# MLP down projection of a one-core layer: the seven block products as the outer loop, sums kept in PSUM, operand sums stored by the up stage

## The chip, the cores and the metric

The kernel runs on one core of a Trainium2 chip. The metric is the time of one execution on the device, in microseconds (us); three runs of the kernel before took 1432.04, 1435.4 and 1437.7 us, a median of 1435.4 us.

## The reference, cut to what matters

One layer over 1024 tokens of width 1024: an attention group and an mLSTM group share an input projection, their outputs go through one output projection, then an MLP of width 4096 and a gated embedding (PLE) follow, and a final norm.

```python
h = h + mix @ w_out[layer]
u = rms_norm(h, norm_mlp_g[layer])
h = h + jnp.square(jax.nn.relu(u @ w_up[layer])) @ w_down[layer]
gate = jax.nn.sigmoid(rms_norm(h, norm_ple_g[layer]) @ w_ple_gate[layer])
h = h + gate * (p[layer] @ w_ple[layer])
return rms_norm(h, final_norm_g)
```

## The kernel before, in words

Everything lies feature-major: a tile is 128 features by 1024 tokens, or by one half of them (512, `CH`). Each fp32 operand of a matmul is split into a high part (ACT's CAST, line 93, L93) and a low part (DVE's subtraction, L94), and each product is then three matmuls, L102 (high by high), L103 and L104 (`mm3`). A matmul is 128x128 by 512 columns.

The stages that matter here follow each other on PE in this order. The **out-projection** (tile `o`) has a first half on the attention output (`mixa`) and a second half on the mLSTM output (`mixm`, weights `wo_r`, loaded at L735 by `load_t`). The second half finishes `h[k]` feature block by feature block, stores it (L846, `hs<-h`), adds its square to `state` (L807/808) and scales it (L848). From the scaled `h`, `operands` makes the operands `x` of the up stage, four plain blocks and four sums `t` that POOL makes (L789). The **PLE product** `pl` (96 matmuls, operand `pp` from the load `pr` at L829) is independent of all that. `rstd_rows` turns `state` into a row factor: a column sum on PE (`cs`, L125), DVE (`ra`, L134), a power on POOL (`rb`, L135 and L823), a broadcast on PE (`bp`, L131), a copy on ACT (`rB`, L814).

The **up stage** (tile `u`, 1344 matmuls) and the **down stage** (tile `d`, 1344 matmuls) replace the eight block products of a 2x2 by 2x2 block matrix product by seven (Strassen-Winograd): `OPS = b11, t1, t2, b22, t3, b21, t4`. This needs sums of weight blocks, which POOL makes in `load_blocks` (L752 to 754) from a load of 512 KB (L751), and sums of operand blocks (`operands`). In the up stage, per pair of feature blocks `f` (16 of them), the result is `zz`: additions on DVE (L895), relu and scaling (L897), squaring on ACT (L898), and a store to DRAM of 1 MB (`zd<-zz`, L899).

The down stage loops over eight groups `g` of 512 hidden features, reads them back (`zr<-zd`, L870), makes the operand sums on POOL and the splits on ACT and DVE, and inside over four pairs of output blocks `o`. Each of the seven products of a pair `(g, o)` is six matmuls in a PSUM bank that is then added into `h` by DVE (L927, 208 times; 16 more go through ACT L924 and POOL L925). After the last group come `state` and the splits `hp` (L96/97), `rstd_rows` once more, and the **PLE gate** (tile `pg`, 456 matmuls, weights `wpg_r`), its evacuations (L947 to 950), the final norm and the output.

The order on each engine is set by a scheduler that runs over the recorded instructions; each engine then executes its list in order, and a DMA issue that waits on SP holds back all later issues of SP.

Of the kernel before, what the change touches and what calls it, by code (L numbers as in the profile page):

```python
# [9 lines left out]
F32 = mybir.dt.float32  # L10
# [35 lines left out]
def layer_kernel(ctx, tc, xT, wqk, wv, wvg, wmv, wmqk, wmo, wout, wup, wdown, wpg, wple, pT,  # L46
# [97 lines left out]
    zd = dram.tile([FF // P // 2, P, 2, T], F32, name="zd")  # L144
# [569 lines left out]
    with ExitStack() as tail:  # L714
        zp = tail.enter_context(tc.tile_pool(name="zp", bufs=2, reuse_waits="tile"))
        wta, wtb, wtc = [tail.enter_context(tc.tile_pool(name="wt" + n, bufs=2, reuse_waits="tile"))
                         for n in "abc"]
        pmm = tail.enter_context(tc.tile_pool(name="pmm2", bufs=6, space=PSUM, reuse_waits="tile"))

        def ztile(name, dt=F32):  # L720
            return zp.tile([P, 2, T], dt, name=name, tag="z", bufs=3)
# [4 lines left out]
        def acc_tile(name, tag="mm"):  # L726
            return pmm.tile([P, CH], F32, name=name, tag=tag, bufs=6 if tag == "mm" else 2)
# [5 lines left out]
        def load_t(src, name, n=KT * P, hl=None):  # L733
            raw = wtc.tile([P, 8 * L], F32, name=name + "_r", tag="wc")
            nc.sync.dma_start(raw[:, :n], src)  # L735
            hl = hl or [t.rearrange("p a b -> p (a b)") for t in wtile(name, 4, "wb")]
            return split([t[:, :n] for t in hl], raw[:, :n])
# [64 lines left out]
        def ssq(state, src, first, eng=V):  # L802
# [5 lines left out]
            eng.tensor_tensor(state, state, sq, op=ALU.add)  # L808

        def rows(dst, c):  # L810
            for j in range(NCH):
                bp = acc_tile("bp2", "x")
# [3 lines left out]
        def rstd_rows(state, times=None):  # L816
            cs = acc_tile("cs2", "x")
# [13 lines left out]
        state, scale = pair("state", F32)  # L831
# [8 lines left out]
        for k in range(KT):  # L840
# [6 lines left out]
            ssq(state, h[k], k == 0)  # L847
# [4 lines left out]
        rB = rstd_rows(state, srec)  # L852
# [13 lines left out]
        def hidden(f, halves=None):  # L866
            if halves is None:
                z = ztile("zr")
                halves = z[:, 0], z[:, 1]
                nc.sync.dma_start(z, zd[f])  # L870
            else:
                for i in range(2):
                    nc.sync.dma_start(halves[i], zd[f, :, i])
            return halves

        OWN = (0, 14, 15)
        for f in range(FF // P // 2):
            if f == FF // P // 2 - 2:
                ahead = [hidden(0), hidden(1, [unit("zr", F32) for _ in range(2)])]
# [19 lines left out]
            nc.sync.dma_start(zd[f], z)  # L899
# [3 lines left out]
        BY_POOL, POOL_O = ("t4",), (1, 2)  # L903
        hp = []
        count[0] = 0

        def operand():
            count[0] += 1
            return pair("y") if count[0] % 9 else (unit("y"), unit("y"))

        for g in range(NG):
            src = ahead if g == 0 else [hidden(2 * g + u) for u in range(2)]
            Y = operands(src, operand, lambda n: unit(n, F32))
            if g == 0:
                h = [unit("h", F32) for _ in range(KT)]
                for k in range(KT):
                    nc.sync.dma_start(h[k], hs[k])
            for o in range(KT // 2):
                def ev(key, ps):
                    i, c = dict(b11=(0, 0), t1=(1, 1), t2=(0, 1), b22=(0, 1), t3=(1, 1), b21=(0, 0), t4=(1, 0))[key]  # L920
                    to = h[2 * o + i][:, c * CH:(c + 1) * CH]
                    if key in BY_POOL and o in POOL_O:
                        t = small("t")
                        S.copy(t, ps)  # L924
                        G.tensor_tensor(to, to, t, op=ALU.add)  # L925
                    else:
                        V.tensor_tensor(to, to, ps, op=ALU.add)  # L927
                products([load_blocks(wdown[g, o], "wd")], [Y], ev, "d")
                if g == NG - 1:
                    for k in (2 * o, 2 * o + 1):  # L930
                        if k == 0:
                            state = pair("state", F32)[0]
                        ssq(state, h[k], k == 0, G if o < 3 else V)
                        hp.append(split((unit("hp"), unit("hp")) if k in (2, 3) else pair("hp"),
                                        h[k], col[:, C_GPLE + k:C_GPLE + k + 1]))
        rB = rstd_rows(state)


# [22 lines left out]
        def final(i, sl):  # L961
            n = sl.stop - sl.start
            nt = n // P
            cs = acc_tile("cs3", "x")
# [8 lines left out]
            bp = acc_tile("bp3", "x")  # L973
# [3 lines left out]
            for k in range(KT):  # L977
                m = 2 * T // n
                if k % m == 0:
                    outs = ztile("out").rearrange("p a (b t) -> p (a b) t", t=n)  # L980
# [14 lines left out]
        TO = ((4, 8), (4, 8), (2, 4, 6, 8))  # L995
        ws = {}

        def fetch(k):
            if k % 2 == 0:
                e = ztile("e")  # L1000
                nc.sync.dma_start(e, ed[k // 2])
                emb[k], emb[k + 1] = e[:, 0], e[:, 1]
            ws[k] = load_t(wpg[k], "wpg", hl=pair("wpg") if k == KT - 1 else None)

        for k in range(KT - LATE):
# [91 lines left out]
```

## Time and profile before

| what | value |
|---|---|
| median of 3 runs | 1435.4 us (1432.04 to 1437.7) |
| the profiled execution: own time / span | 1431.62 us / 1429.8 us |
| busy, share of the span: PE, DVE, ACT, POOL | 95%, 73%, 44%, 38% |
| PE busy | 1353.3 us, 6815 matmuls |
| traffic | 157.91 MB, mean 110 GB/s |
| chain that ended last, by engine | PE 44%, DVE 13%, POOL 8%, DMA 5%, issue 4% |

The span is the stretch that the profiler recorded; the own time is what the same execution took on the device. A matmul's duration in a row (about 0.39 us) is longer than its pitch, since matmuls overlap in the pipeline; the pitch is the distance of two starts. In the rows of a timeline the bracket at the end is the idle time of that engine before the instruction, and what ended it. The granted clock (PEclk) is a share of the full 2.4 GHz.

### The profile page before, as it was taken

The page shows a single profiled execution, that of the slowest core. Times are in us where ns is not written, and L with a number is a line of the kernel's source. Part 1 is how long each engine was busy: PE and PEld are TensorE (multiplying, and loading weights), DVE is VectorE, ACT ScalarE, POOL GpSimd, SP SyncE. Part 2 cuts the span into 40 slices and gives each one's busy share as a digit, 9 for nine tenths or more (in the row PEclk, how much of TensorE's full clock was granted, in tenths as well). Part 3 has the DMA queues.
Part 4 walks back from the last instruction along what each step waited for, and adds up shares of the span by engine and source line. Part 5 has one row for each costly group of instructions (what it writes and reads, how often), then busy time and mean ns, then how long its engine had stood idle before and what let it go on. Part 6 is the DMA issues. An engine that isn't in the chain of part 4 may idle for free.

```text
span 1429.8 us, 18360 instructions
## 1 busy us (share of the span) xinstructions
PE 1353.3 (95%) x6815; PEld 1123.4 (79%) x6815; DVE 1043.3 (73%) x1603; ACT 628.0 (44%) x1007; POOL 548.0 (38%) x395
## 2 busy tenths in 40 slices
PE   8999999999979999998999999997999899999996
PEld 6978988978868887777888888885777777777885
DVE  6788689599758894784444444459988899998666
ACT  6455645644455352355344333443433334335332
POOL 1532121141113220263332233348766878746002
PEclk9999999999999999999999999999999999999998
DMA  6111012222144368442432223446323133221403
GB/s 225 45 49 38 23 48 73 60 77 97 60 147 137 108 211 291 159 162 103 147 118 103 98 94 118 148 148 236 118 96 110 59 104 103 74 59 60 161 30 118
DMA packets 54233, 157.91 MB, mean 110 GB/s; under 512 B 5664, under 2 KB 15808, under 8 KB 49152
## 3 DMA queue, kind: packets, MB, share of 16 engines
q1 hardware_dynamic: 54144, 156.75, 32.4%
q8 instruction: 53, 0.87, 0.3%
q14 instruction: 36, 0.29, 0.1%
HBM read 113.19 MB, written 43.54 MB: 110 GB/s over the span
## 4 chain that ended last, share of the span: by engine, by line
PE 44%; DVE 13%; POOL 8%; DMA 5%; issue 4%; ACT 2%; SPq 0%; DVEq 0%; POOLq 0%; ACTq 0%
PE u L102 7%; PE u L103 7%; PE u L104 6%; POOL t L789 3%; PE d L102 2%; DVE h L927 2%; PE d L104 2%; DVE wdl L94 2%; PE d L103 2%; POOL wd_r L752 2%; PE pg L104 2%; PE pg L102 2%; PE pg L103 2%; DVE y L94 2%; DMA wd_r<-wdown 2%
## 5 line engine op out<-in xcount | busy, mean ns | idle before, releaser
L102 PE MATMUL d<-y,wdh 128*128 128x512 f32 x448 | 179.2, 403 | 18.9 <-DVE h L927 13.4
L94 DVE TENSOR_TENSOR wul<-wu_r,wuh 128x768 fp32r<-128x768 f32 (+1 forms) x64 | 75.3, 1178 | 148.9 <-ACT wuh L93 148.7
L103 PE MATMUL d<-y,wdh 128*128 128x512 f32 x448 | 178.1, 398 | 1.1 <-DVE y L94 1.1
L103 PE MATMUL u<-x,wuh 128*128 128x512 f32 x448 | 175.2, 395 | 0.0
L104 PE MATMUL d<-y,wdl 128*128 128x512 f32 x448 | 170.0, 400 | 4.9 <-DVE wdl L94 4.8
L102 PE MATMUL u<-x,wuh 128*128 128x512 f32 x448 | 172.3, 395 | 0.0
L104 PE MATMUL u<-x,wul 128*128 128x512 f32 x448 | 171.2, 394 | 0.0
L927 DVE TENSOR_TENSOR h<-h,d 128x512 f32<-128x512 f32 x208 | 132.9, 676 | 3.5 <-PE d L104 3.1
L752 POOL TENSOR_TENSOR wu_r<-wu_r 128x512 f32<-128x512 f32 x32 | 44.9, 1403 | 207.9 <-DMA wu_r<-wup 151.7
L102 PEld LDWEIGHTS d<-y,wdh 128*128 128x128 f32 x448 | 85.2, 190 | 47.0 <-DVE h L927 19.4
L93 ACT CAST wdh<-wd_r 128x1024 fp32r<-128x1024 f32 (+1 forms) x64 | 58.9, 942 | 130.8 <-POOL wd_r L753 89.4
L94 DVE TENSOR_TENSOR wdl<-wd_r,wdh 128x1024 fp32r<-128x1024 f32 (+1 forms) x64 | 89.5, 1404 | 26.0 <-ACT wdh L93 26.0
L104 PEld LDWEIGHTS d<-y,wdl 128*128 128x128 f32 x448 | 85.1, 190 | 28.1 <-DVE wdl L94 8.1
L103 PEld LDWEIGHTS d<-y,wdh 128*128 128x128 f32 x448 | 85.2, 190 | 20.8 <-DVE y L94 1.5
L104 PEld LDWEIGHTS u<-x,wul 128*128 128x128 f32 x448 | 84.7, 189 | 19.9
L103 PEld LDWEIGHTS u<-x,wuh 128*128 128x128 f32 x448 | 84.6, 189 | 19.9
L102 PEld LDWEIGHTS u<-x,wuh 128*128 128x128 f32 x448 | 84.5, 189 | 19.5
L93 ACT CAST wuh<-wu_r 128x768 fp32r<-128x768 f32 (+1 forms) x64 | 60.2, 942 | 74.9 <-POOL wu_r L753 45.7
L752 POOL TENSOR_TENSOR wd_r<-wd_r 128x512 f32<-128x512 f32 x32 | 49.6, 1552 | 72.0 <-DMA wd_r<-wdown 58.4
L412 ACT ACTIVATE pr<-pr,mn 128x128 f32<-128x128 f32 (+3 forms) x64 | 49.5, 774 | 54.6 <-PE av L415 30.4
L887 ACT COPY tmp<-u 128x512 f32<-128x512 f32 x48 | 28.0, 586 | 95.1 <-PE u L104 95.1
L407 DVE CUSTOM_DVE_ANT_0 pr<-s,biasS 128x512 f32<-128x512 f32 (+2 forms) x96 | 51.1, 550 | 12.5 <-PE tp L422 8.9
(363 smaller groups left out, 3712.1 us busy)
## 6 DMA issues: line engine op xcount, KB each, us to landing
wu_r<-wup SPq DMA_DIRECT2D x32, 512.0 KB
zd<-zz SPq DMA_DIRECT2D x16, 1024.0 KB
wd_r<-wdown SPq DMA_DIRECT2D x32, 512.0 KB
zr<-zd SPq DMA_DIRECT2D x15, 1024.0 KB
wm_r<-wmqk SPq DMA_DIRECT2D x8, 512.0 KB
wo_r<-wout SPq DMA_DIRECT2D x16, 256.0 KB
hs<-h SPq DMA_DIRECT2D x8, 512.0 KB
ed<-emb SPq DMA_DIRECT2D x4, 1024.0 KB
```

Source lines behind the costliest of these rows:

```text
L93: S.copy(hi, src)
L94: V.tensor_tensor(lo, src, hi.bitcast(F32), op=ALU.subtract)
L102: PE.matmul(ps, wh, xh, start=start, stop=False, skip_group_check=more)
L103: PE.matmul(ps, wh, xl, start=False, stop=False, skip_group_check=more)
L104: PE.matmul(ps, wl, xh, start=False, stop=stop, skip_group_check=more)
L407: V.tensor_tensor_reduce(pr[:, ks], s[:, :n], biasS[:, b0 + o:b0 + o + n], 1.0, -2 * LOW, op0=ALU.add, op1=ALU.min, accum_out=mn[:, o // C ...
L412: S.activation(pr[:, :nk], pr[:, :nk], AF.Exp, scale=-1.0, bias=mn[:, :1], accum_out=den)
L752: G.tensor_tensor(raw[:, 4:7:2], raw[:, 2:3].to_broadcast([P, 2, L]), raw[:, 1:4:2], op=ALU.subtract)
L789: G.tensor_tensor(ts[key][:, us], src[u][i0][:, s0], in1, op=o)
L887: S.copy(tmp[key], ps)
L927: V.tensor_tensor(to, to, ps, op=ALU.add)
```

## The change

The up stage computes the four operand sums of the down stage itself, on DVE, and stores them beside `z` (8 slots of half a token row per feature block instead of 2 rows of whole tokens). The down stage turns its loops round: the seven products are the outer loop, the eight groups the inner one, and per step it loads one operand tile `y_r` (512 KB) and one or two weight blocks `wd_r` (512 KB each, two for `t1` and `t3`), makes one weight sum on POOL for four of the seven products, splits both, and issues 24 matmuls into four PSUM banks. A bank collects its sums over all eight groups and is added into `h` only at the last (28 times). `state`, `hp` and the row factor are made for each half of the tokens, the second half's (`rstd_half(1)`) after `t3`. The out tiles and loads of the PLE gate take their buffers from the pools of the down stage. The pools before the down stage are laid out anew: `wtc` (raw weights of the out-projection and the up stage) comes right behind the small tiles, and `wtc`, `zu`, `wta` and `wtb` are closed after the up stage, so that the buffers of the down stage lie where they were. PSUM has one pool of eight banks in place of six and two.

```diff
-    zd = dram.tile([FF // P // 2, P, 2, T], F32, name="zd")
+    zd = dram.tile([FF // P // 2, P, 8, CH], F32, name="zd")
...
-        wta, wtb, wtc = [tail.enter_context(tc.tile_pool(name="wt" + n, bufs=2, reuse_waits="tile"))
-                         for n in "abc"]
-        pmm = tail.enter_context(tc.tile_pool(name="pmm2", bufs=6, space=PSUM, reuse_waits="tile"))
+        up_scope = ExitStack()
+        wtc, zu, wta, wtb = [up_scope.enter_context(tc.tile_pool(name=n, bufs=2, reuse_waits="tile"))
+                             for n in ("wtc", "zu", "wta", "wtb")]
+        pmm = tail.enter_context(tc.tile_pool(name="pmm2", bufs=8, space=PSUM, reuse_waits="tile"))
...
-            nc.sync.dma_start(zd[f], z)
+            nc.sync.dma_start(zd[f, :, :4], z.rearrange("p a (c t) -> p (a c) t", t=CH))
+            ts = ztile("zt").rearrange("p a (c t) -> p (a c) t", t=CH)
+            c0, c1 = slice(0, CH), slice(CH, T)
+            V.tensor_tensor(ts[:, 0], z[:, 0, c1], z[:, 0, c0], op=ALU.subtract)
+            V.tensor_tensor(ts[:, 1], z[:, 1, c1], ts[:, 0], op=ALU.add)
+            V.tensor_tensor(ts[:, 2], z[:, 0, c1], z[:, 1, c1], op=ALU.add)
+            V.tensor_tensor(ts[:, 3], z[:, 1, c0], ts[:, 1], op=ALU.subtract)
+            nc.sync.dma_start(zd[f, :, 4:], ts)
+        up_scope.close()
...
-        for g in range(NG):
-            src = ahead if g == 0 else [hidden(2 * g + u) for u in range(2)]
-            Y = operands(src, operand, lambda n: unit(n, F32))
...
-            for o in range(KT // 2):
...
-                        V.tensor_tensor(to, to, ps, op=ALU.add)
-                products([load_blocks(wdown[g, o], "wd")], [Y], ev, "d")
...
-        rB = rstd_rows(state)
+        rawp, hlp = [tail.enter_context(tc.tile_pool(name=n, bufs=3, reuse_waits="tile")) for n in ("rawp", "hlp")]
...
+        def parts(name, tag, src):
+            return split([hlp.tile([P, T], F32R, name=name + i, tag=tag + i) for i in "hl"], src)
+
+        def wraw(g, blk):
+            r = stream("wd_r", "wr", 4)
+            nc.sync.dma_start(r, wdown[g, blk])
+            return r
...
+        def weights(key, g):
+
+            if key in ("b11", "b21", "t4"):
+                return wraw(g, dict(b11=A11, b21=A12, t4=A22)[key])
+            if key == "t1":
+                a, b = wraw(g, A21), wraw(g, A22)
+                G.tensor_tensor(sw[g], a, b, op=ALU.subtract)
+            elif key == "t3":
+                a, b = wraw(g, A21), wraw(g, A11)
+                G.tensor_tensor(a, a, b, op=ALU.subtract)
+                return a
+            else:
+                a = wraw(g, dict(t2=A11, b22=A12)[key])
+                G.tensor_tensor(sw[g], a, sw[g], op=ALU.subtract)
+            return sw[g]
...
+        def ready(k, c):
+
+            sl = slice(c * CH, (c + 1) * CH)
+            if k == 0:
+                S.activation(state[:, sl], h[k][:, sl], AF.Square)
+            else:
+                sq = small("sq")
+                S.activation(sq, h[k][:, sl], AF.Square)
+                G.tensor_tensor(state[:, sl], state[:, sl], sq, op=ALU.add)
+            split((hp[k][0][:, sl], hp[k][1][:, sl]), h[k][:, sl], col[:, C_GPLE + k:C_GPLE + k + 1])
...
+        for key in OPS:
...
+            for g in range(NG):
+                y = stream("y_r", "yr", 3)
+                nc.sync.dma_start(y.rearrange("p (f t) -> p f t", t=CH),
+                                  zd[2 * g:2 * g + 2, :, SLOT[key]].rearrange("f p t -> p f t"))
+                yh, yl = parts("y", "y", y)
+                wh, wl = parts("wd", "w", weights(key, g))
+                for o in range(KT // 2):
+                    for u in range(2):
...
+                        mm3(ps[o], wh[:, at], wl[:, at], yh[:, us], yl[:, us],
+                            fresh and g == 0 and u == 0, g == NG - 1 and u == 1, not fresh)
+                    if g == NG - 1:
+                        to = h[2 * o + i][:, c * CH:(c + 1) * CH]
+                        V.tensor_tensor(to, to, ps[o], op=ALU.add)
+                        if key in DONE:
+                            ready(2 * o + i, c)
+            if key == "t3":
+                rstd_half(1)
+        rstd_half(0)
```

The order of the two programs at three places, engine by engine:

**Between the out-projection and the up stage.** SP's list before, around the load `pr` of the PLE operand; `wo_r` are the weights of the second half of the out-projection, `hd` and `in` its other traffic:

```order
L735 DMA wo_r<-wout 128x512 x2
L667 DMA hd<-t 128x512
L665 DMA t<-xT 128x512 x2
L667 DMA hd<-t 128x512
L844 DMA h<-hd 128x1024
L735 DMA wo_r<-wout 128x512
L540 DMA in<-mixmd 128x512
L735 DMA wo_r<-wout 128x512
L667 DMA hd<-t 128x512
L540 DMA in<-mixmd 128x512
L667 DMA hd<-t 128x512
L829 DMA pr<-pT 128x2x1024
```

and now:

```order
L845 DMA h<-hd 128x1024
L540 DMA in<-mixmd 128x512
L667 DMA hd<-t 128x512 x2
L830 DMA pr<-pT 128x2x1024
L736 DMA wo_r<-wout 128x512 x4
L847 DMA hs<-h 128x1024
```

The first four loads of `wo_r` stood ahead of `pr` and stand behind it now; the first of them now also waits for the last matmul of the first half, whose weights lie in the same place.

PE's list before, at the end of the PLE product `pl`; `cs` and `bp` are the column sum and the broadcast of the row factor:

```order
L104 MATMUL pl<-pp,wpll 128x512
L125 MATMUL cs_6614<-ones,state 128x1 x8
L102 MATMUL pl<-pp,wplh 128x512
...
L131 MATMUL bp_6629<-ident,rb 128x128 x4
L131 MATMUL bp_6635<-ident,rb 128x128 x4
L102 MATMUL pl<-pp,wplh 128x512
L103 MATMUL pl<-pp,wplh 128x512
L104 MATMUL pl<-pp,wpll 128x512
L102 MATMUL pl<-pp,wplh 128x512
L103 MATMUL pl<-pp,wplh 128x512
L104 MATMUL pl<-pp,wpll 128x512
L102 MATMUL u<-x,wuh 128x512
```

and now:

```order
L104 MATMUL o<-mixm,wol 128x512
L125 MATMUL cs_6617<-ones,state 128x1 x8
L131 MATMUL bp_6632<-ident,rb 128x128 x4
L131 MATMUL bp_6638<-ident,rb 128x128 x4
L102 MATMUL pl<-pp,wplh 128x512
L103 MATMUL pl<-pp,wplh 128x512
L104 MATMUL pl<-pp,wpll 128x512
```

Before, all but six of the 96 matmuls of `pl` stood ahead of `bp`; now `cs` and `bp` stand right behind the out-projection, and all 96 behind them.

**Between the up and the down stage.** SP's list before, at the last store of `zz`:

```order
L751 DMA wd_r<-wdown 128x1024 x2
L899 DMA zd<-zz 128x2048
L917 DMA h<-hs 128x1024 x5
L870 DMA zr<-zd 128x2048
L917 DMA h<-hs 128x1024 x3
L870 DMA zr<-zd 128x2048
L751 DMA wd_r<-wdown 128x1024 x2
L899 DMA zd<-zz 128x2048
```

and now:

```order
L937 DMA h<-hs 128x1024 x3
L888 DMA zd<-zz 128x2048
L895 DMA zd<-zt 128x2048
L977 DMA y_r<-zd 128x2x512
L911 DMA wd_r<-wdown 128x1024
L977 DMA y_r<-zd 128x2x512
L911 DMA wd_r<-wdown 128x1024
```

The first loads of the down stage stood ahead of the last store of the up stage; now both of its last stores stand ahead of every load of the down stage.

**Inside and behind the down stage.** PE's list now, at the end of `t3`, the fifth of the seven products, and at the end of the seventh:

```order
L104 MATMUL d<-yh,wdl 128x512
L125 MATMUL cs_10527<-ones,state 128x1 x4
L131 MATMUL bp_10536<-ident,rb 128x128 x4
L102 MATMUL d<-yh,wdh 128x512
...
L104 MATMUL d<-yh,wdl 128x512
L125 MATMUL cs_11168<-ones,state 128x1 x4
L131 MATMUL bp_11177<-ident,rb 128x128 x4
L102 MATMUL pg<-hp,wpgh 128x512
```

and before, at the end of the down stage:

```order
L102 MATMUL pg<-hp,wpgh 128x512
L125 MATMUL cs_11347<-ones,state 128x1 x8
L103 MATMUL pg<-hp,wpgh 128x512
...
L131 MATMUL bp_11361<-ident,rb 128x128 x4
L131 MATMUL bp_11367<-ident,rb 128x128 x4
```

Before, matmuls of the PLE gate stood ahead of the last ones of `d`, ahead of `cs` and between `cs` and `bp`. Now a `cs` and `bp` stand in the midst of the down stage, with nothing between them, and the others stand ahead of the first matmul of the gate.

## Rows read from the trace of the kernel before

**Rows 1.** Page, groups: line engine op out<-in, shapes, count | busy us, mean ns | idle before, releaser

```profile
L102 PE MATMUL d<-y,wdh 128*128 128x512 f32 x448 | 179.2, 403 | 18.9 <-DVE h L927 13.4
...
L102 PE MATMUL u<-x,wuh 128*128 128x512 f32 x448 | 172.3, 395 | 0.0
...
L927 DVE TENSOR_TENSOR h<-h,d 128x512 f32<-128x512 f32 x208 | 132.9, 676 | 3.5 <-PE d L104 3.1
...
L94 DVE TENSOR_TENSOR wdl<-wd_r,wdh 128x1024 fp32r<-128x1024 f32 (+1 forms) x64 | 89.5, 1404 | 26.0 <-ACT wdh L93 26.0
```

**Rows 2.** Tile d: ns min/median/max, first and last start in us, forms

```profile
L102 PE MATMUL d<-y,wdh x448: 387/393/796, 968.2 to 1324.8; 128*128 128x512 f32 x150
...
L104 PE MATMUL d<-y,wdl x448: 388/393/792, 968.7 to 1325.2; 128*128 128x512 f32 x150
```

**Rows 3.** Windows: stretch, length, busy us (count) of each engine, PEclk, DMA share, GB/s

```profile
640.00:655.00 15.00, 9.74 (x38) 7.53 (x38) 5.42 (x7) 10.66 (x18) 12.41 (x11) 0.82 0.42 176
...
675.00:968.20 293.20, 293.20 (x1263) 237.72 (x1262) 136.72 (x125) 121.16 (x141) 101.35 (x95) 1.00 0.34 121
```

**Rows 4.** Windows, the DMA at its busiest, same columns

```profile
550.00:560.00 10.00, 8.51 (x40) 6.61 (x39) 6.56 (x10) 3.05 (x5) 0.00 (x0) 1.00 0.91 314
560.00:570.00 10.00, 10.00 (x45) 8.19 (x44) 3.99 (x6) 1.86 (x3) 0.00 (x0) 1.00 0.96 316
```

**Rows 5.** Timeline of SP at the out-projection: start us, us, engine line op

```profile
557.95 1.30 SPq L735 DMA_DIRECT2D wo_r<-wout  x2
...
575.73 0.38 SPq L829 DMA_DIRECT2D pr<-pT  x1
584.82 0.32 SPq L846 DMA_DIRECT2D hs<-h  x1
```

**Rows 6.** Timeline of ACT, same stretch: idle time and its releaser in brackets

```profile
580.75 2.00 ACT L93 CAST pp<-pr 128x1024 fp32r<-128x1024 f32 x2 [6.55 <-DMA pr<-pT]
...
583.61 0.63 ACT L93 CAST woh<-wo_r 128x512 fp32r<-128x512 f32 x1
```

**Rows 7.** Timeline of DVE, first and last feature block of the second half

```profile
587.76 1.28 DVE L848 SCALAR_TENSOR_TENSOR h<-h,col,state 128x1024 f32<-128x1024 f32 x1 [1.30 <-DMA hs<-h]
...
633.81 1.21 DVE L808 TENSOR_TENSOR state<-state,sq 128x1024 f32<-128x1024 f32 x1
```

**Rows 8.** Timeline of POOL ahead of the up stage

```profile
637.42 3.08 POOL L752 TENSOR_TENSOR wu_r<-wu_r 128x512 f32<-128x512 f32 x1 [5.76 <-DVE x L94]
640.46 1.29 POOL L789 TENSOR_TENSOR t<-h,t 128x512 f32<-128x512 f32 x1
...
647.32 2.09 POOL L135 TENSOR_TENSOR rb<-ra,mhalf 128x8 f32<-128x8 f32 x1
...
650.80 0.20 POOL L823 TENSOR_TENSOR rb<-rb,srec 128x8 f32<-128x8 f32 x1
```

**Rows 9.** Timeline of PE, end of the out-projection to the up stage

```profile
621.59 0.39 PE L104 MATMUL o<-mixm,wol 128*128 128x512 f32 x1
...
651.06 1.97 PE L131 MATMUL bp<-ident,rb 128*128 128x128 f32 x8 [4.65 <-POOL rb L823]
...
654.10 0.63 PE L102 MATMUL pl<-pp,wplh 128*128 128x512 f32 x1
...
655.38 0.63 PE L102 MATMUL u<-x,wuh 128*128 128x512 f32 x1
```

**Rows 10.** Tile zz, the two last steps of the up stage's result

```profile
L897 DVE SCALAR_TENSOR_TENSOR zz<-zz,rB x16: 2283/2284/3376, 682.0 to 985.1; 128x2048 f32<-128x2048 f32 x16
L898 ACT ACTIVATE zz<-zz x16: 1911/1918/1921, 687.0 to 988.5; 128x2048 f32<-128x2048 f32 x16
```

**Rows 11.** Chain of waits in the down stage: start us, us, what

```profile
1022.13 4.71 DMA zr<-zd
```

**Rows 12.** Tile pg up to 1325.3 us, columns as in group 2

```profile
L102 PE MATMUL pg<-hp,wpgh x9: 390/395/404, 1315.7 to 1323.8; 128*128 128x512 f32 x9
```

**Rows 13.** Timeline of POOL, the power over half the tokens

```profile
1404.56 1.17 POOL L972 TENSOR_TENSOR rb<-ra,mhalf 128x4 f32<-128x4 f32 x1 [67.19 <-DVE ra L971]
```

More of the change, by code (lines that the diff above doesn't have):

```diff
@@ L800, in operands, with ssq @@
             return x
-        def ssq(state, src, first, eng=V):
+        def ssq(state, src, first):
             if first:
@@ L807, in ssq @@
             S.activation(sq, src, AF.Square)
-            eng.tensor_tensor(state, state, sq, op=ALU.add)
+            V.tensor_tensor(state, state, sq, op=ALU.add)
         def rows(dst, c):
             for j in range(NCH):
-                bp = acc_tile("bp2", "x")
+                bp = acc_tile("bp2")
                 bcast_rows(bp, c[:, j * NB // 2:(j + 1) * NB // 2], NB // 2)
@@ L830, in layer_kernel @@
         pp = [split(pair("pp"), pr[:, k]) for k in range(PLE // P)]
-        state, scale = pair("state", F32)
+        sqs, scale = pair("state", F32)
         rows(scale, scol)
@@ new lines, in layer_kernel @@
+        A11, A12, A21, A22 = range(4)
+        SLOT = dict(b11=0, b21=2, b22=3, t1=4, t2=5, t3=6, t4=7)
+        sp4 = [pair("s", F32) for _ in range(NG // 2)]
+        sw = [sp4[g // 2][g % 2] for g in range(NG)]
+        def weights(key, g):
[12 more added lines that the diff above has]
+            return sw[g]
@@ new lines, in layer_kernel @@
+        h = [unit("h", F32) for _ in range(KT)]
+        for k in range(KT):
+            nc.sync.dma_start(h[k], hs[k])
+        state = unit("state", F32)
+        hp = [pair("hp") for _ in range(KT)]
+        rB = zp.tile([P, T], F32, name="rB", tag="rB", bufs=1)
+        TO_C = dict(b11=(0, 0), t1=(1, 1), t2=(0, 1), b22=(0, 1), t3=(1, 1), b21=(0, 0), t4=(1, 0))
+        DONE = dict(b22=(0, 1), t3=(1, 1), b21=(0, 0), t4=(1, 0))
+        def ready(k, c):
[7 more added lines that the diff above has]
+            split((hp[k][0][:, sl], hp[k][1][:, sl]), h[k][:, sl], col[:, C_GPLE + k:C_GPLE + k + 1])
@@ new lines, in rstd_half @@
+        def rstd_half(c):
+            sl = slice(c * CH, (c + 1) * CH)
+            n = NB // 2
+            cs = acc_tile("cs2")
+            col_sum(cs, state[:, sl], n=n)
+            a = zp.tile([P, NB], F32, name="ra", tag="ra")
+            b = zp.tile([P, NB], F32, name="rb", tag="rb")
+            V.tensor_scalar(a[:, :n], cs[:, :n], 1.0 / D, EPS, op0=ALU.mult, op1=ALU.add)
+            G.tensor_tensor(b[:, :n], a[:, :n], mhalf[:, :n], op=ALU.pow)
+            bp = acc_tile("bp2")
+            bcast_rows(bp, b, n)
+            S.copy(rB[:, sl], bp)
@@ L994, in layer_kernel @@
         ON_V = ((0, 3, 6), range(KT), (0, 2, 3, 5, 6, 7))
-        TO = ((4, 8), (4, 8), (2, 4, 6, 8))
+        TO = ((2, 4, 6, 8), (4, 8), (2, 4, 6, 8))
         ws = {}
         def fetch(k):
[L999 to L1005, printed above, removed]
+            emb[k] = stream("e", "yr", 3)
+            nc.sync.dma_start(emb[k], ed[k // 2, :, k % 2])
+            r = stream("wpg_r", "wr", 4)
+            nc.sync.dma_start(r, wpg[k])
+            ws[k] = split((unit("wpg"), unit("wpg")), r) if k == KT - 1 else parts("wpg", "w", r)
+        for k in range(2):
+            fetch(k)
+        for c in (1, 0):
+            for k in range(2):
+                embed(ws[k], k, slice(c * CH, (c + 1) * CH))
+        for k in range(2, KT - LATE):
             fetch(k)
@@ L1082 @@
         "wmo": tiles(w_in[:, 3072:3584]), "wout": tiles(a["w_out"][0]), "wup": wu[:, :, :, order],
[L1083 removed]
+        "wdown": wd, "wpg": tiles(a["w_ple_gate"][0]), "wple": wpl,
         "pT": a["p"][0, 0].T.reshape(2, P, T), "cols": cols, "cosT": cosT, "sinT": sinT, "biasT": bias,
```

75 lines of the change are left out of this document (24 added, 51 removed).

## Prediction

> **What bounds the kernel now.** I read the page first: PE is busy 95% of the span, so a change pays only where PE waits, and costs wherever PE is made to wait. The groups of the page [rows 1] say where it waits now: the matmuls of the up stage have no idle time in front of them (0.0), those of the down stage have 18.9 us in front of L102 alone, most of it put down to DVE's additions into `h`, 208 of 0.676 us. The tile view [rows 2] gives the stage its length: `d` starts at 968.2 and its last matmul at 1325.2, with one pitch more 357.2 us. The windows [rows 3] give the pitch of a PE that lacks nothing: 293.20 us busy of 293.20, 1263 matmuls, 0.232 us each. 1344 matmuls at that pitch are 312.0 us, so **45 us** lie in the down stage to be had, and nothing more.
>
> The rest of the reading is about joints. The kernel before has work on PE across each of them: the PLE product under the row factor before the up stage, the down stage's first loads under the last of the up stage, gate matmuls under the second row factor. The timelines of PE, ACT, DVE and POOL give the durations of the chains that this work hides [rows 5 to 10].
>
> **The down stage: -45.** A step is now 24 matmuls, 24 x 0.232 = 5.57 us. Beside it DVE has two low-part subtractions of 128x1024, 1.404 us on average where POOL and DVE disturb each other [rows 1], and additions into `h` only at every eighth step; ACT two casts of 1.0 us [rows 6]; POOL in four of seven products one sum of 128x1024, twice the 1.29 us of a half [rows 8]. All are under 5.57. The loads are 56 operand tiles and 72 weight blocks of 0.5 MB, 128 x 0.524 = 67 MB in 312 us, 215 GB/s on average, and 1.57 MB per step (282 GB/s) in `t1` and `t3`; the DMA moved 314 and 316 GB/s at a share of 0.91 to 0.96 [rows 4]. It fits, closely in `t1` and `t3`. I take the whole 45. Bounds: -45 and -25 (first rival).
>
> The Trainium skill, DMA: Bandwidth & Descriptors, speaks against the transfers: its section Anatomy of one DMA gives a fixed 2.0 us to every transfer and its section Bandwidth asks for 1 MiB or more; the change replaces operand loads of 1 MB by loads of half that. By that price a transfer of 512 KB would take some 3.2 us (an estimate from that page, which measured another way of issuing), and 128 of them one after another 410 us. The windows with 314 GB/s are made of transfers of 256 and 512 KB, so the fixed part overlaps there; the rule decides only if the new loads do not overlap.
>
> **From the out-projection to the up stage: +27.** In the order of the program two things move. (a) `pr` is ahead of every `wo_r`, and PE can't begin the second half without one. `pr` was issued at 575.73 [rows 5] and used at 580.75 [rows 6], 5.0 us later; the wait for the last split of `mixm` that it has now ended some 0.8 us sooner, so it lands near 579.9. ACT then has two casts (2.00), one copy and the first `woh` cast (0.63) in its list; before, the same with two copies ended at 584.2 [rows 6]. With 0.8 us less of waiting and a copy of some 0.5 less, the second half starts near 583, where before two `wo_r` had been issued at 557.95 and ACT, PE and DVE had begun long before `pr` came. 24 matmuls (5.6), some 2 us for the slower clock after the pause (below), an addition (0.7) and the store of `hs` (2.9, from its issue at 584.82 [rows 5] to L848, which waited for it) put the first L848 at 594.5 instead of 587.76 [rows 7]: +7. Bounds 0 (DVE catches up) and +9.
>
> (b) `state` was complete at 633.81 + 1.21 = 635.0 [rows 7]; POOL then worked through weight and operand sums from 637.42, began the power at 647.32 and ended the row factor at 651.0 [rows 8]; `bp` began at 651.06 after 4.65 us of idle PE, and `u` at 655.38 [rows 9]. 33.8 us passed from the last `o` to the first `u`, and 22.3 of them (96 x 0.232) were `pl`. Now all of `pl` comes behind `bp`, so this chain covers nothing. The sums ahead of the power stay in POOL's list but for one. So: row factor at 651.0 + 7 - 1.3 = 656.7, `bp` to 658.3, `pl` 22.3 and 2 for the clock: `u` at 682.6, **+27**. Bounds: +20 (no shift from a) and +31.
>
> The clock: in 640 to 655 us the granted clock was 0.82 [rows 3], a mixture of 2.4 and 1.2 GHz, and after the pause of 4.65 us three matmuls took 1.28 us (654.10 to 655.38), 0.43 each, almost twice 0.232 [rows 9]. At 0.82 the lower level held 5.4 of the 15 us. I charge 2 us for each new pause of that size.
>
> **The up stage: 0.** DVE gets 16 x 4 half-tile operations of about 0.68, 43 us on top of 136.72 in 293.2 us [rows 3]; the second store adds 16.8 MB, some 54 GB/s on 121, against 314. PE's slack covers both. If it doesn't: +5.
>
> **Between up and down: +19.** PE went from `u` to `d` without a pause: 0.2 us of pitch. Now SP holds both last stores ahead of the first load. From the last `u`: addition 0.8, L897 2.28, L898 1.92 [rows 10], four half-tile operations 2.7, and hand-overs: the `zt` store is issued at about 8.0, `y_r` at 8.4, `wd_r` at 8.7. 1 MB took 4.71 us from issue to landing [rows 11]. With nothing in the way the first step's two loads land near 12.4; behind the two stores, 2 MB and their own 1 MB at 314 GB/s, near 17. Two casts of 1.0 us, and 2 for the clock: 16.4 to 21. I take 19, since the `zz` store is mostly through when the loads are issued; the low bound is 14 (no clock loss).
>
> **Inside the down stage, after `t3`: +10.** A row factor for half the tokens stands in PE's list between two products, with no matmul between `cs` and `bp`. From the last matmul of `t3` ACT's list has a cast that waits for that same matmul, a square and a split of the third block, another such cast and only then the last square: 1.0 + 0.6 + 0.6 + 1.0 + 0.6 = 3.8. Then POOL's addition 1.29 [rows 8], `cs` 0.8 (half of what eight take, from `bp` [rows 9]), `ra` 0.2, the power 1.17 [rows 13], `bp` 0.8: 8.1, and 2 for the clock. Bounds 5 and 12.
>
> **Behind the down stage: +12.** The same chain with one cast in it is about 6.1 us. Before, 25 gate matmuls (9 of L102 [rows 12], 8 each of L103 and L104) ran before `d` ended, 5.8 us that now come after it; the clock is 2; `cs` and `bp` of before, some 2 us of PE in that stretch, come off. Bounds 8 and 15. From there to the end I change nothing.
>
> **Sum.** 27 + 0 + 19 + 10 + 12 - 45 = **+23**. On the profiled span of 1429.8 us that is 1453, on its own time of 1431.62 us 1455. The three runs shown have a median of 1435.4 us, 3.8 above the profiled execution; I put the forecast between the two frames, at **1457 us**. A difference under 0.5%, about 7 us, is about what a measurement of this kernel can't tell from none. The lower bounds together make +2, the upper ones +39, and +59 if the down stage gains 25 only.
>
> **Rivals.** *The down stage is held by its operands (slower still).* In `t1` and `t3` two of the four raw buffers go into each step, so a pair comes round every two steps, 11.1 us. Its round: landing of 1 MB 4.7 [rows 11], the sum 2.6, cast 1.0, low part 1.4: 9.7; but POOL's first row before the up stage took 3.08 for a half of 1.29 [rows 8], and with such a POOL the sum alone is 6 us. That makes up to 2 us per pair, 16 steps: +8 to +20; the middle gives 1457 + 12 = **1469**. For it: the DMA's share would be 0.9. Against: the average POOL row is nearer to 1.3. Chance 0.17.
>
> *The row factor comes early (not slower).* Ten of the 16 us from `state` to `bp` are POOL's queue [rows 7, 8]. If POOL is through its sums when `state` is done, and DVE catches up the 7 us of (a), 17 us come off: 1457 - 17 = **1440**, no difference that can be told. It decides if `pl` begins by 642, some 12 us behind a last out-projection matmul near 630 (583 + 2 + 192 x 0.232); before, `bp` began 29 us behind it [rows 9]. For it: POOL idled 5.76 us before 637.42. Against: what it waited for is a split on DVE, which is as late as the rest. Chance 0.10.
>
> *The loads don't overlap.* By the figure of the Trainium skill, DMA: Bandwidth & Descriptors, section Anatomy of one DMA, this would add about 100 us (128 x 3.2 less 312). By rows: half of the 4.71 us of 1 MB is the least a load of 512 KB could take alone, 301 us in all and no loss, and the full 4.71 makes 603 us, 1457 + 290 = **1747**. Against it stand the windows of 314 GB/s [rows 4]. Chance 0.03. That the change does not take the waits of `d` away for another reason, for instance because they were those of splits (26.0 us idle before DVE's `wdl` [rows 1]), would cost up to 20 of the 45: 1477, chance 0.03.
>
> **Numbers.** My case has 0.67, and by itself 1446 to 1468. 1440 to 1476 takes in most of the first rival and the edge of the second; outside stay the far ends. Faster than 1428: 0.05, from all low bounds and a little overlap that I don't see. Within 0.5% (1428 to 1442.6): 0.09. Slower: 0.86.
>
> **What would show it.** Right: matmuls of `d` at 0.232 us with almost no idle time in front of L102 and 28 additions in place of 208; a PE row of `bp` some 27 us behind the last `o` and the first `u` near 683; 15 to 19 us of idle PE between `u` and `d`, ended by a cast that waited for `y_r` or `wd_r`; idle time of about 8 and 6 us in front of `cs` and `bp` in the midst of `d` and behind it, with a clock under 1.0 after each. Wrong: `u` before 670; a `d` that starts within 10 us; or matmuls of `d` in `t1` and `t3` waiting for POOL or the DMA.

## The result, and the profile after

The changed kernel takes 1451.7 us (median of 4 runs, 1451.09 to 1452.87), the kernel before 1435.02 us (4 runs); the ratio is 1.0118, 95% interval 1.0096 to 1.0139. It is **slower by 1.2%**. The profiled span went from 1429.8 to 1449.3 us, 19.5 us more.

Cut at the first and last matmuls of the stages, the two spans compare so:

| from, to | before, us | after, us | difference |
|---|---|---|---|
| start to the first `u` | 655.4 | 681.3 | +25.9 |
| first `u` to the first `d` | 312.8 | 329.6 | +16.8 |
| first `d` to the end of the last | 357.2 | 319.4 | -37.8 |
| from there to the end of the last `pg` | 87.8 | 105.1 | +17.3 |
| to the end of the span | 16.6 | 13.9 | -2.7 |

The down stage did give what was looked for. The joints around it, and one in its midst, took that back and more. The page's groups after, in the columns of [rows 1]:

```profile
L102 PE MATMUL d<-yh,wdh 128*128 128x512 f32 x448 | 176.5, 394 | 17.1 <-ACT wdh L93 17.1
...
L102 PE MATMUL u<-x,wuh 128*128 128x512 f32 x448 | 174.3, 395 | 0.0
...
L94 DVE TENSOR_TENSOR wdl<-s,wdh 128x1024 fp32r<-128x1024 f32 x24 | 54.1, 2255 | 24.5 <-ACT wdh L93 24.5
```

In front of L102 of `d` 17.1 us are left, all of them one pause that a cast ended; the waits for DVE's additions are gone. DVE's low parts of the weight sums got slow, 2.255 us on average (18 of the 24 have POOL at work beside them; the six that don't took 1.22 to 1.23), but a step of 5.4 us has room for one of these and for the operand's low part, and no matmul waits for them. Tile `d` after, to be held against [rows 2]:

```profile
L102 PE MATMUL d<-yh,wdh x448: 388/389/795, 1010.9 to 1329.6; 128*128 128x512 f32 x150
...
L104 PE MATMUL d<-yh,wdl x448: 387/389/628, 1014.5 to 1330.1; 128*128 128x512 f32 x150
L989 DVE TENSOR_TENSOR h<-h,d x28: 673/677/689, 1053.8 to 1330.5; 128x512 f32<-128x512 f32 x28
```

There are 28 additions on DVE instead of 208. The windows after, with the columns of [rows 3], show where PE does not work:

```profile
640.00:655.00 15.00, 3.57 (x16) 3.49 (x16) 11.39 (x12) 5.00 (x7) 11.59 (x7) 0.50 0.10 37
...
681.30:993.60 312.30, 312.30 (x1345) 253.06 (x1343) 197.82 (x192) 125.82 (x147) 106.18 (x87) 1.00 0.44 166
993.60:1011.00 17.40, 0.28 (x2) 0.05 (x1) 7.42 (x9) 4.15 (x4) 0.00 (x0) 0.66 0.65 235
...
1022.00:1231.00 209.00, 209.00 (x922) 172.63 (x921) 156.30 (x100) 82.41 (x87) 101.44 (x36) 1.00 0.70 236
1231.00:1247.00 16.00, 8.70 (x32) 7.08 (x31) 8.45 (x9) 5.69 (x9) 6.74 (x5) 0.68 0.36 110
...
1330.30:1345.00 14.70, 8.79 (x30) 7.26 (x30) 6.56 (x7) 3.70 (x6) 5.52 (x4) 0.65 0.11 39
...
1422.00:1430.00 8.00, 6.50 (x45) 6.41 (x44) 4.48 (x10) 3.87 (x7) 5.04 (x5) 0.79 0.21 78
```

Read the first figure of each engine group against the length: PE is full in the up stage (312.30 of 312.30) and in the down stage up to the end of `t3` (209.00 of 209.00, 922 matmuls), and it is 3.57 of 15.00, 0.28 of 17.40, 8.70 of 16.00 and 8.79 of 14.70 in four joints, with a granted clock of 0.50 to 0.68. A smaller pause lies in the gate (6.50 of 8.00, clock 0.79). The same places in PE's timeline, with the start of the second half of the out-projection ahead of them; the bracket at the end is the idle time and what ended it:

```profile
581.77 0.50 PE L102 MATMUL o<-mixm,woh 128*128 128x512 f32 x1 [3.72 <-ACT woh L93]
...
641.96 3.57 PE L125 MATMUL cs<-ones,state 128*128 128x1 f32 x16 [13.38 <-DVE state L809]
655.47 1.97 PE L131 MATMUL bp<-ident,rb 128*128 128x128 f32 x8 [9.93 <-POOL rb L824]
...
1010.95 0.80 PE L102 MATMUL d<-yh,wdh 128*128 128x512 f32 x1 [17.12 <-ACT wdh L93]
...
1231.26 0.39 PE L104 MATMUL d<-yh,wdl 128*128 128x512 f32 x1
1237.60 1.87 PE L125 MATMUL cs<-ones,state 128*128 128x1 f32 x8 [5.95 <-POOL state L952]
1240.82 1.12 PE L131 MATMUL bp<-ident,rb 128*128 128x128 f32 x4 [1.35 <-POOL rb L963]
1241.59 0.78 PE L102 MATMUL d<-yh,wdh 128*128 128x512 f32 x1
1242.16 0.63 PE L103 MATMUL d<-yl,wdh 128*128 128x512 f32 x1
...
1335.02 1.87 PE L125 MATMUL cs<-ones,state 128*128 128x1 f32 x8 [4.56 <-POOL state L952]
1338.23 1.11 PE L131 MATMUL bp<-ident,rb 128*128 128x128 f32 x4 [1.35 <-POOL rb L963]
...
1424.77 0.65 PE L131 MATMUL bp<-ident,rb 128*128 128x128 f32 x4 [1.50 <-POOL rb L1030]
```

One by one: the second half of the out-projection waits for its first weights; behind it the column sum waits 13.38 us for `state` and the broadcast 9.93 us for POOL, with no matmul of `pl` to run meanwhile; `d` waits 17.12 us for its first cast; after `t3` PE is done at 1231.5 and begins `b21` at 1241.59; after the last `d` the column sum waits 4.56 us for POOL's last addition; and the broadcast of the final norm waits 1.50 us, where the kernel before had gate matmuls between its `cs` (1403.34) and `bp` (1407.91). Two matmuls after the pause behind `t3` start 0.43 us apart (1242.16 to 1242.59; at a granted clock of 1.00 it is 0.227), which is the 1.2 GHz level instead of 2.4. SP's and ACT's timelines between `u` and `d` show the order of the lists at work, the loads behind the two stores and the casts behind the loads:

```profile
999.41 0.32 SPq L888 DMA_DIRECT2D zd<-zz  x1
1002.07 0.32 SPq L895 DMA_DIRECT2D zd<-zt  x1
1002.48 0.42 SPq L977 DMA_DIRECT2D y_r<-zd  x1
```

```profile
1008.67 1.04 ACT L93 CAST yh<-y_r 128x1024 fp32r<-128x1024 f32 x1 [9.28 <-DMA y_r<-zd]
1009.85 1.04 ACT L93 CAST wdh<-wd_r 128x1024 fp32r<-128x1024 f32 x1
```

### The profile page after: what moved, and what is told of

Read it like the earlier page. It is cut to its first block, busy times and chain, and to the rows that moved or that the text cites. A ratio compares the mean times of both kernels' runs of the same rounds, so it can differ in the third digit from the quotient of the medians.

```text
span 1449.3 us, 18272 instructions
## 1 busy us (share of the span) xinstructions
PE 1350.0 (93%) x6815; PEld 1135.3 (78%) x6815; DVE 987.5 (68%) x1462; ACT 621.9 (43%) x975; POOL 415.3 (29%) x261
## 4 chain that ended last, share of the span: by engine, by line
PE 52%; DVE 9%; issue 8%; DMA 4%; POOL 2%; ACT 2%; SPq 0%; DVEq 0%; ACTq 0%; POOLq 0%
PE u L102 7%; PE u L103 7%; PE u L104 7%; PE d L102 7%; PE d L103 7%; PE d L104 7%; DMA in<-mixmd 1%; POOL state L952 1%; PE pl L103 1%; PE pl L102 1%; PE pl L104 1%; PE cs L125 1%; PE mo L102 1%; DMA wo_r<-wout 1%; PE mo L103 1%
## 5 line engine op out<-in xcount | busy, mean ns | idle before, releaser
L102 PE MATMUL d<-yh,wdh 128*128 128x512 f32 x448 | 176.5, 394 | 17.1 <-ACT wdh L93 17.1
L103 PE MATMUL d<-yl,wdh 128*128 128x512 f32 x448 | 176.3, 393 | 0.0
L104 PE MATMUL d<-yh,wdl 128*128 128x512 f32 x448 | 174.4, 391 | 0.0
L102 PE MATMUL u<-x,wuh 128*128 128x512 f32 x448 | 174.3, 395 | 0.0
L102 PEld LDWEIGHTS d<-yh,wdh 128*128 128x128 f32 x448 | 85.2, 190 | 35.4 <-ACT wdh L93 17.6
L102 PEld LDWEIGHTS u<-x,wuh 128*128 128x128 f32 x448 | 84.4, 188 | 19.7
L103 PEld LDWEIGHTS d<-yl,wdh 128*128 128x128 f32 x448 | 85.2, 190 | 18.4 <-DVE yl L94 0.6
L104 PEld LDWEIGHTS d<-yh,wdl 128*128 128x128 f32 x448 | 84.9, 189 | 17.7
L94 DVE TENSOR_TENSOR yl<-y_r,yh 128x1024 fp32r<-128x1024 f32 x56 | 92.3, 1648 | 8.0 <-ACT yh L93 7.9
L94 DVE TENSOR_TENSOR wdl<-wd_r,wdh 128x1024 fp32r<-128x1024 f32 x32 | 44.8, 1399 | 70.5 <-ACT wdh L93 70.4
L94 DVE TENSOR_TENSOR wdl<-s,wdh 128x1024 fp32r<-128x1024 f32 x24 | 54.1, 2255 | 24.5 <-ACT wdh L93 24.5
L93 ACT CAST yh<-y_r 128x1024 fp32r<-128x1024 f32 x56 | 58.7, 1048 | 12.3 <-DMA y_r<-zd 10.0
```

The lines of the kernel that those rows point to most:

```text
L93: S.copy(hi, src)
L94: V.tensor_tensor(lo, src, hi.bitcast(F32), op=ALU.subtract)
L102: PE.matmul(ps, wh, xh, start=start, stop=False, skip_group_check=more)
L103: PE.matmul(ps, wh, xl, start=False, stop=False, skip_group_check=more)
L104: PE.matmul(ps, wl, xh, start=False, stop=stop, skip_group_check=more)
```

## The experiments

Each is an edit of the changed kernel. "Less" is against the changed kernel, by the two ratios to the kernel before, times 1435 us.

**The row factor one product later.**

```diff
-            if key == "t3":
+            if key == "b21":
                 rstd_half(1)
```

> The row factor of the second half of the tokens is made one product later (behind b21 instead of behind t3). Theory of the joints: PE's pause behind t3 (from 1231.5 to the first matmul of b21 at 1241.6, and the slower clock until 1245) goes, since POOL has the whole of b21 for the last addition: 10 to 12 us less than the changed kernel, about 1441, and idle time in front of cs of nearly 0 there. Rival (the down stage is held by its operands): PE would only wait for casts and loads at b21 instead, under 4 us gained, about 1449.

1441.6 us, ratio 1.0044 (1.0027 to 1.0062), 10.6 us less. PE's timeline has `cs` and `bp` among the matmuls of the sixth product, with no idle time in front of them, and `cs` takes 0.95 us there instead of 1.87:

```profile
1279.45 0.95 PE L125 MATMUL cs<-ones,state 128*128 128x1 f32 x8
...
1286.73 0.60 PE L131 MATMUL bp<-ident,rb 128*128 128x128 f32 x4
```

So the pause came from the place in the list, and the gain lies in the range expected. The rival falls: `b21` did not wait for its operands instead.

**The PLE product ahead of the row factor.**

```diff
-        rB = rstd_rows(sqs, srec)
         for k2 in range(KT // 2):
...
             nc.sync.dma_start(ed[k2], e)
+        rB = rstd_rows(sqs, srec)
```

> The PLE product is written ahead of the row factor, so that its 96 matmuls stand ahead of cs and bp in PE's list, as before. Theory of the joints: it covers the chain from state to bp again, the first u comes at about 658 to 660 instead of 681.3: 21 to 23 us less than the changed kernel, about 1430. Rival (the later start of the second half of the out-projection is the cost, the place of pl matters little): the first u stays near 675, 5 us gained, about 1447.

1438.4 us, ratio 1.0023 (1.0005 to 1.0041), 13.6 us less; the first `u` at 665.2. Neither number was met. PE's, DVE's and POOL's timelines say why:

```profile
651.02 1.84 PE L125 MATMUL cs<-ones,state 128*128 128x1 f32 x16
663.53 1.97 PE L131 MATMUL bp<-ident,rb 128*128 128x128 f32 x8 [10.67 <-POOL rb L824]
```

```profile
659.78 0.16 DVE L134 TENSOR_SCALAR ra<-cs 128x8 f32<-128x8 f32 x1
```

```profile
655.58 0.72 POOL L755 TENSOR_TENSOR wu_r<-wu_r 128x256 f32<-128x256 f32 x1
660.02 2.56 POOL L135 TENSOR_TENSOR rb<-ra,mhalf 128x8 f32<-128x8 f32 x1 [3.71 <-DVE ra L134]
```

Now the column sum stood behind all 96 matmuls, 10 us after `state` was there; then DVE had splits ahead of `ra` in its list, so that POOL, free from 656.3 on, waited 3.71 us for it, and PE 10.67 for POOL. It is not enough to put matmuls over a chain; its first link must stand early as well. Hence the next run.

**The column sum behind 72 of the 96.**

```diff
-            dst = zp.tile([P, T], F32, name="rB", tag="rB", bufs=1)
-            rows(dst, b)
-            return dst
+            return b
...
-        rB = rstd_rows(sqs, srec)
...
+            if k2 == 2:
+                rb = rstd_rows(sqs, srec)
+        rB = zp.tile([P, T], F32, name="rB", tag="rB", bufs=1)
+        rows(rB, rb)
```

> As with the PLE product ahead of the row factor, where the column sum stood behind all 96 matmuls and began at 651.0, though state was done at 641.3; now it stands behind 72 of them. Theory of the joints: POOL's power no longer waits for a late column sum, but for the sums in its list up to 656.3; the first u comes at 660 to 661 instead of 665.2, 18 to 21 us less than the changed kernel, about 1432. Rival (POOL's and DVE's queues set it, not the column sum): u stays at 664 to 666, about 1438.

1432.6 us, ratio 0.9988 (0.9971 to 1.0005), 18.7 us less; the first `u` at 658.7, 22.6 us earlier than in the changed kernel. Not all of this is the edit's: the last `o` also came 3.3 us earlier (624.9 instead of 628.2), for a reason ahead of it. From the last `o` to the first `u` passed 53.1 us in the changed kernel and 33.8 here, as in the kernel before: the edit is worth 19.3 (18.7 by the times). The power now follows POOL's sums without a wait:

```profile
653.62 1.05 POOL L755 TENSOR_TENSOR wu_r<-wu_r 128x256 f32<-128x256 f32 x1
654.64 2.09 POOL L135 TENSOR_TENSOR rb<-ra,mhalf 128x8 f32<-128x8 f32 x1
```

With this edit alone the changed kernel is as fast as the one before.

**The first loads of the down stage early.**

```diff
+            if f == FF // P // 2 - 1:
+                nc.scalar.dma_start(zd[f, :, :4], z.rearrange("p a (c t) -> p (a c) t", t=CH))
...
+            if f == FF // P // 2 - 1:
+                for p0 in (0, 64):
+                    nc.gpsimd.dma_start(zd[f, p0:p0 + 64, 4:], ts[p0:p0 + 64])
...
-                yh, yl = parts("y", "y", y)
-                wh, wl = parts("wd", "w", weights(key, g))
+                first = key == "b11" and g == 0
+                yh, yl = split((unit("yh"), unit("yl")), y) if first else parts("y", "y", y)
+                raw = weights(key, g)
+                wh, wl = split((unit("wh"), unit("wl")), raw) if first else parts("wd", "w", raw)
```

> The two stores of the last pair of the up stage are issued by ACT and POOL instead of SP, and the parts of the first step of the down stage lie in tiles that the last stores don't use. Theory of the joints: SP's list and the buffers hold the first loads back; the first d comes at about 1002 instead of 1011, 7 to 9 us less than the changed kernel, about 1444. Rival (the DMA itself is what takes the time, two stores of 1 MB and the loads at its full rate): the first d stays within 3 us of 1011 and the time at 1450.

1444.4 us, ratio 1.0066 (1.0048 to 1.0083), 7.5 us less. SP's and PE's timelines:

```profile
989.93 0.44 SPq L984 DMA_DIRECT2D y_r<-zd  x1
...
991.03 0.50 SPq L984 DMA_DIRECT2D y_r<-zd  x1
1003.92 0.33 SPq L918 DMA_DIRECT2D wd_r<-wdown  x1
```

```profile
1002.36 0.80 PE L102 MATMUL d<-yh,wh 128*128 128x512 f32 x1 [8.02 <-ACT wh L93]
1003.75 0.79 PE L103 MATMUL d<-yl,wh 128*128 128x512 f32 x1 [0.59 <-DVE yl L94]
```

The first load went out 12.5 us sooner and `d` began at 1002.36. Half of the pause was the order of SP's list and the shared buffers. 8.02 us stay: the evacuation and squaring of the last pair, which stand ahead of the first casts on ACT. The fourth load had to wait for the store of the last `zz` all the same (1003.92), and the down stage got 2.6 us longer.

**48 gate matmuls ahead of the last row factor.**

```diff
-        rstd_half(0)
...
             for k in range(2):
                 embed(ws[k], k, slice(c * CH, (c + 1) * CH))
+            if c:
+                rstd_half(0)
```

> 48 gate matmuls of the second half of the tokens are written ahead of the row factor of the first half. Theory of the joints: they cover the 8.7 us from the last d to the first pg, and the slower clock goes with it: 9 to 11 us less than the changed kernel, about 1441. Rival (the gate's weights or the evacuations of the gate hold this stage): the pause moves into the gate and under 4 us are gained, about 1449.

1442.4 us, ratio 1.0058 (1.0038 to 1.0077), 8.6 us less, a little under the 9 to 11 expected. Between the last `d` and the first `pg` lies no pause, and `cs` follows the 48 at once:

```profile
1341.33 0.95 PE L125 MATMUL cs<-ones,state 128*128 128x1 f32 x8
1343.63 1.12 PE L131 MATMUL bp<-ident,rb 128*128 128x128 f32 x4 [1.35 <-POOL rb L963]
```

`bp` still waits 1.35 us, since nothing stands between `cs` and `bp`, and the slower clock did not go altogether: the matmuls behind `bp` start 0.43 us apart again (1344.97 to 1345.39), and the granted clock from 1341 to 1348 was 0.76.

**The PLE operand's load late.**

```diff
-        pr = ztile("pr")
-        nc.sync.dma_start(pr, pT.rearrange("k p t -> p k t"))
-        pp = [split(pair("pp"), pr[:, k]) for k in range(PLE // P)]
...
+            if k == 2:
+                pr = ztile("pr")
+                nc.sync.dma_start(pr, pT.rearrange("k p t -> p k t"))
+                pp = [split(pair("pp"), pr[:, j]) for j in range(PLE // P)]
```

> The load of the PLE operand and its splits are written behind the third feature block, so that the first weights of the second half of the out-projection don't stand behind them on SP and ACT. The prediction's step (a) put 6 us on this place in the lists (second half at 583 instead of 577). If it is right, the second half starts at about 577 to 578 and the time falls by 5 to 6 us, to about 1446. Rival (the weights lie now where the first half's weights lay, and can only be loaded once its last matmul is done at 576.8): it starts near 580.3, 1.5 us sooner than the 581.8 of the changed kernel, and the time stays within 3 us of 1451.

1453.2 us, ratio 1.0134 (1.0112 to 1.0157): no gain. The second half started at 581.6, against 581.77 without the edit. SP's and ACT's timelines, and between them a row of SP's waits from 570 to 600 us (total, times, longest):

```profile
578.21 5.50 SPq L736 DMA_DIRECT2D wo_r<-wout  x4
...
595.93 1.53 SPq L846 DMA_DIRECT2D pr<-pT  x1
```

```profile
SPq L736 <- PE o L104: 5.6, 1, 5.6
```

```profile
580.93 0.62 ACT L93 CAST woh<-wo_r 128x512 fp32r<-128x512 f32 x1 [1.20 <-DMA wo_r<-wout]
```

With `pr` out of the way SP still waits 5.6 us for the last matmul of the first half (it starts at 577.78), issues the weights at 578.21, and the first cast waits for their landing at 580.9. In the changed kernel that matmul started at 576.78 and the weights went out at 577.21. So from their issue to the first matmul it is 3.4 us instead of 4.6, and that the first half ended 1.0 us later here took nearly all of it back. My rival was right about the cause and too hopeful about the start.

**All four joints.** The edits of `factor_late`, `ple_split`, `loads_early` and `gate_first` in one kernel.

> Four edits at once: row factor of the second half behind b21, PLE product split around the column sum, early first loads of the down stage, 48 gate matmuls ahead of the last row factor. Theory of the joints: each pays where it stands, so their gains add: 10 + 19 + 7 + 9 = 45 less than the changed kernel, about 1406, faster than both kernels. Rival (they share one slack, for instance the same DMA or DVE work, that then binds): under 30 together, above 1421.

**1411.2 us**, ratio 0.9842 (0.9826 to 0.9857): 39.6 us less than the changed kernel and 1.6% faster than the kernel before. The single gains add to 45.4; of the 5.8 that are missing, 4.7 are a first `u` at 663.4 instead of 658.7, a delay that is there before the column sum already (DVE's last addition to `state` at 642.16 instead of 637.43). It does not come from the edits at this joint: from the last `o` to the first `u` it is 33.9 us here and 33.8 in `ple_split`, and the last matmul of the first half of the out-projection starts at 577.5 instead of 573.6, so 3.9 of the 4.7 us are there before any edited line runs. Why that first half ends at different times in kernels that share its code is open.

**The pitch of `d`.** 750 matmuls in 170.00 us were 0.2267 us each in the changed kernel, against 0.2325 in `u` of either kernel and in `d` of the kernel before. Where the tiles of `d` lie in a partition: `y` from 169344 to 193919 bytes, the weights `w` from 193920 to 218495. So the operands of `d` do not lie where they did: in the kernel before the streamed ones lay from 1280 to 115967, the weights from 165248 to 193919. Three runs exchanged them with `h` tiles or pools, one execution each (1456.8, 1461.3 and 1451.4 us), and a fourth put both low (1451.0). Of the first of them the one line that matters here:

```diff
...
-                yh, yl = parts("y", "y", y)
+                yh, yl = split(yt[step[0] % 3], y)
...
```

> The matmuls of d have a pitch of 0.2267 us in the changed kernel, those of every other stage and of the kernel before 0.2325. Here the operand tiles of d lie where those of the other stages lie, in the lower part of SBUF, and six of the h tiles in their place; loads of these h tiles come later. If the place of the streamed operand sets the pitch, it goes to 0.2325 and d gets 8 us longer. Rival (it is the form of the loop, 24 matmuls from one pair of tiles without a wait between): it stays at 0.2267. One look, for the pitch alone.

> With the operand tiles in the lower part of SBUF the pitch of d went from 0.2267 to 0.2325. Here the streamed operand tiles stay in the upper part (193920 bytes and up in each partition) and the stationary weight tiles go to the lower part (75008 to 107776); six h tiles change place with them. If the place of the streamed operand alone sets the pitch: 0.2267. Rival (both must lie in the same part): 0.2325. One look, for the pitch alone.

> Two pools of the down stage change place, so that the streamed operand tiles lie at 140672 to 165247 and the weights at 165248 to 189823 bytes of each partition, instead of 169344 to 193919 and 193920 to 218495. If any place above the 124160 bytes where the other stages' operands end gives the shorter pitch: 0.2267. Rival (only the topmost part does): 0.2325. One look, for the pitch alone.

> With either the streamed operand or the weights of d in the lower part of SBUF the pitch was 0.2325 (0.2323 to 0.2333), with both in the upper part 0.2267. Here both lie in the lower part (66816 to 124160 bytes of each partition); h and state lie where they were. If it is enough that both lie in one part: 0.2267. Rival (only the upper part gives the shorter pitch): 0.2325. One look, for the pitch alone.

Windows of `d` in the four kernels, in this order (streamed operands low; weights low; both high in other places; both low):

```profile
1060.00:1200.00 140.00, 140.00 (x604) 113.47 (x603) 110.12 (x64) 54.67 (x59) 82.92 (x28) 1.00 0.67 219
```

```profile
1060.00:1200.00 140.00, 139.30 (x598) 112.24 (x598) 111.66 (x66) 53.74 (x57) 80.74 (x27) 1.00 0.67 221
```

```profile
1030.00:1200.00 170.00, 169.99 (x750) 140.47 (x750) 133.24 (x81) 68.05 (x72) 92.73 (x32) 1.00 0.68 226
```

```profile
1030.00:1200.00 170.00, 169.22 (x746) 139.66 (x745) 141.72 (x83) 69.90 (x73) 94.70 (x32) 1.00 0.72 244
```

By single matmuls that is 0.2325, 0.2325, 0.2267 and 0.2267 us. Neither the place of the streamed tiles alone nor that of the weights alone sets it, nor the form of the loop, which all four share: with one of the two below 124160 bytes and the other from 193920 up the pitch is 0.2325, with both below 124160 or both above 140672 it is 0.2267. The PLE gate, whose streamed operands `hp` lie below 67840 in the kernels with the new loops, bears this out. With its weights from 165248 up its matmuls of 512 columns started 0.2314 to 0.2327 us apart; in the fourth run, where these weights lie low too, 0.2262. Its last weight block lies low in every kernel, the one before included, and there it was 0.2267 to 0.2284. The theory that the streamed tiles alone set it fell with the second run, the rival that only the upper part will do with the fourth. Where the border lies, or whether it is the distance that counts, these placements don't tell.

## Why the prediction was right, and where not

Forecast were 1457 us (1440 to 1476) and slower; measured were 1451.7 and slower, with an interval of the ratio that lies wholly above 1. By its steps:

- **The down stage, -45: mis-sized, -52.5.** The mechanism held (no wait for additions, operands always there, no rival by the DMA: 236 GB/s at a share of 0.70 and PE full). But I took the pitch of the up stage, 0.232. It was 0.2267, so the matmuls alone took 304.7 us (1344 times the pitch), 52.5 less than before. 45 of that is the waits that the new loops took away; the other 7.5 is the place of the tiles, as the runs on the pitch show, and the prediction had no term for it. The rule of the Trainium skill, DMA: Bandwidth & Descriptors (section Bandwidth), that transfers want 1 MiB or more, did not decide: some 49 MB (236 GB/s for 209 us, 1022 to 1231) came in transfers of 512 KB, with no pause of PE.
- **To the first `u`, +27: 25.9.** Step (b) was right in mechanism and size: POOL's power ended the factor, all of `pl` came behind it, and from the last `o` to the first `u` passed 53.1 us instead of 33.8, 19.3 more (I had 20). Step (a) was right in size by luck (L849 of the first block 5.5 us later; I had 7). The cause was mostly not `pr` ahead of the weights but the weights' place, which is free only after the first half's last matmul; `pr_late` shows that. Besides, that matmul came 1.2 us later than before (576.78, was 575.54).
- **The up stage, 0:** first to last `u` took 312.3 us, before 312.8.
- **Between `u` and `d`, +19: 16.8 and some 3 in the first steps.** The pause was 17.1; `loads_early`, where 8.02 were left, shows that the lists and buffers made half of it.
- **After `t3`, +10: about 11.7**, 10.1 of pause and 1.6 by the clock; `factor_late` took 10.6 off.
- **Behind `d`, +12: 17.3, mis-sized.** The chain was 8.7 instead of 6.1 us: POOL's four additions queued behind each other, and after 4.56 us of idleness PE ran `cs` in 1.87 us, for which I had 0.8 (0.95 in the run without a pause). The other 2.7 lie in the gate, where I had changed nothing. 1.50 of them are the pause in front of `bp` of the final norm (1424.77); behind it the clock was low again (0.59 from 1425 to 1429, 24 matmuls in 4.00 us where the kernel before had 37 from 1403 to 1407), which by these counts costs some 1.4.
- **The end, 0: -2.7**, not expected. No run isolates it, and the cause is open.

The errors of -7.5 and +5.3 cancel in part, and the forecast had put 2 to 4 us on top of the sum for the time itself; that it came within 5.3 us is partly luck.

The rivals: once begun, the down stage did not wait for operands (PE full from 1022 to 1231, `t1` and `t3` among it); the row factor did not come early by itself, and the run that moved its column sum shows what the joint is worth, 19.3 us; the loads overlapped (236 GB/s).

## What to carry to other kernels

Before a loop is turned round to free one engine, list what the old loop hid at its joints: here 52 us came off a stage, 7.5 of them by where its tiles happen to lie, and 75 us came into the open (25.9, 19.8, 11.7 and 17.3), most of it chains and pauses that other work had covered. Such a chain cost no pause in `factor_late`, where independent matmuls stood behind its first link and ahead of its last in PE's list, so look at the order of the built program for every `cs`/`bp` pair with nothing in between. Three small moves of that kind, and loads issued ahead of the last stores, turned a change that lost 1.2% into one that gains 1.6%.

## What the runs showed of the hardware that was not expected

A matmul of 128x128 by 512 columns took 0.2325 us from start to start with one operand below 124160 bytes of a partition and the other from 165248 up, and 0.2267 us with both below 124160 or both above 140672, 2.5% less, at a granted clock of 1.00; `d` in six kernels and the PLE gate agree. The Trainium skill, TensorE: Matmul & The Clock Gate (Part 1: The HAM clock gate), has 215.7 ns for 512 columns back to back at the full clock; both pitches here lie above it.

A short pause cost twice: after idle times of 4.56 and 5.95 us the small matmuls of `cs` ran 1.87 us instead of 0.95, and they stand on the very chain that PE was waiting for. The clock also fell where PE had only `cs`, a wait of 1.35 or 1.50 us and `bp` to run: 0.76 (`gate_first`, 1341 to 1348) and 0.79 (the changed kernel, 1422 to 1430).
